# A recurrent layer's small weights: resident in plain fp32 instead of reloaded and split, and the spill of low parts moved to another issuing engine

## The chip, the cores and the metric

The kernel runs on one core of one Trainium2 chip. The metric is the device time of one execution in microseconds (us), the median of three runs of the kernel. A profile is one further execution with the hardware profiler on; its span (first to last instruction) lies inside its own time, and all durations and waits below come from that one execution.

The engines are named as the profile names them: PE is the matrix engine (PEld its weight loads), DVE, ACT and POOL are the three elementwise engines, SP issues transfers. ACT issues transfers as well, and those stand in its own instruction stream, between its computations. Every engine takes its instructions strictly in its own order: an instruction that waits for a semaphore holds everything behind it.

## The reference, cut to what matters

Two layers run over 1024 tokens of width 1024: first RWKV-7 time mixing, then sparse attention, each followed by a gated feed-forward part. The change touches only the first:

```python
xx = token_shift(x) - x
xm = x[None] + xx[None] * mix[:, None, None, :]
r, k, v = jnp.einsum('nbsd,nde->nbse', xm[:3], w_rkv)
xw, xa, xg = xm[3], xm[4], xm[5]
w_log = -jax.nn.softplus(-(w0 + jnp.tanh(xw @ w1) @ w2)) - 0.5
decay = jnp.exp(-jnp.exp(w_log.astype(f32)))
a = jax.nn.sigmoid(a0 + (xa @ a1) @ a2)
g = jax.nn.sigmoid(xg @ g1) @ g2
...
_, y = lax.scan(_wkv7_step, state0, xs)
```

`w2` and `a2` are the second low-rank weights: 64 rows by 1024 columns each. All of it is fp32.

## The kernel before, in words

**Products.** An fp32 operand of a large product is split into a high part (a cast to fp32r) and a low part (operand minus high part); `mm3` (L63) then makes one product out of three fp32r matmuls, high·high, high·low and low·high. Each split is one cast on ACT (L54) and one subtraction on DVE or POOL (L60). A plain fp32 matmul is also possible and needs no split; in the trace it stands as two matmul records for each instruction.

**The recurrent layer** (`rwkv`, L307) handles four units: two halves of 512 tokens (hf 0 and 1) times two groups of 512 channels (g 0 and 1). For a unit come, by the list `CFG['order']` at L867: the transposed input and the first low-rank products (`load_x`, `lora1`, once for each half), the second low-rank products (`lora2`), the projections r, k and v (`rproj`, `kproj`, `vproj`), the decays, the preparation and inversion of the chunks (`prep`, `invert`), and the recurrence over eight chunks (`wkv`). The recurrence of one unit is interleaved with the projections of the next; the first unit's projections have no recurrence beside them. A scheduler of the language then fixes the order on each engine from these calls.

**A projection** (`proj`, L471) runs over eight blocks of 128 input channels (kt 0 to 7). For each it needs the split weight block (`wh`, `wl`) and the split mixed input (`xmh`, `xml`), 128x512 each, and makes 12 matmuls of 512 columns: four output tiles times three. `pair` (L440) decides where operands come from. What is needed again is spilled to DRAM when it is first made and loaded when it is needed again: weights in hf 0 (`kept_w`), mixed inputs at g = 0 (`kept_xm`). So the first unit makes and spills both, the second makes and spills weights and loads mixed inputs, the third loads weights and makes and spills mixed inputs, the fourth only loads. A block moves 256 KB in each transfer: in the first unit one load and four spills. Both spills of a pair are issued by ACT (L451), high part then low part.

**Buffers.** Raw weight blocks pass through three tiles (`raw`, L395). All split operands pass through one ring of `k.NU` tiles (`u`, L317), 14 of 128x512: a tile is free for its next owner when its matmuls have run and its spill has landed. Four PSUM tiles (`acc`, L326) hold the outputs of a projection or of the low-rank products.

**`lora1`** (L398) makes four first low-rank products and from them `hw` (tanh, split: high part in rows 0 to 63, low part in rows 64 to 127) and `ha` (rows 0 to 63 and 64 to 127 as well), three DVE and three ACT instructions for the two. **`lora2`** (L500) loads the group's halves of `w2` and `a2` (stored twice, one copy for each 64 rows, so 128 rows each), splits them, and for each of four blocks of 128 channels makes two products of two 128-row fp32r matmuls (L517, L518) and applies a sigmoid on ACT (L519). It runs four times, once for each unit.

**Names in the rows below.** `pa` is the PSUM output of a projection, `la` of a first and `l` (`l2`) of a second low-rank product; `wr` is a raw weight block; `xm` the mixed input before its split; SPq and ACTq are the transfer issues of SP and ACT.

Of the kernel before, what the change touches and what calls it, by code (L numbers as in the profile page):

```python
# [7 lines left out]
F32 = mybir.dt.float32  # L8
F32R = mybir.dt.float32r
BF16 = mybir.dt.bfloat16  # L10
AF = mybir.ActivationFunctionType
ALU = mybir.AluOpType
# [12 lines left out]
V_MIX, V_W0, V_A0, V_KK, V_KA, V_RK = 0, 48, 56, 64, 72, 80  # L25
# [20 lines left out]
def f32(ap):  # L46
    return ap.bitcast(F32)
# [72 lines left out]
def wsplit(k, u, ap, n=512, lo_eng="v", raw=None):  # L120

    raw = (raw or u)("wr")[:, :n]
    lo, hi = u("wl", F32R)[:, :n], u("wh", F32R)[:, :n]
    k.nc.sync.dma_start(raw, ap)
    split(k, raw, hi, lo, "a", lo_eng)
    return hi, lo
# [180 lines left out]
def rwkv(k, src, dst):  # L307
    nc, tc = k.nc, k.tc
    E = lambda n: nc.vector if CFG[n] == "v" else nc.gpsimd
    pools = Pools(tc)  # L310
    P_, M_ = pools.add("rw", first=True, side="left"), pools.add("rwm", side="left")
# [5 lines left out]
    def u(name, dt=F32):  # L317
        return P_.tile([128, 512], dt, name=name, tag="u", bufs=k.NU)

    def t(name, dt=F32):  # L320
        return M_.tile([128, 512], dt, name=name, tag="t", bufs=5)
# [4 lines left out]
    def acc(name):  # L326
        return PS.tile([128, 512], F32, name=name, tag="acc", bufs=4)
# [25 lines left out]
    SB = [M_.tile([128, 4, 2, 64], F32, name=f"S{g}") for g in range(2)]  # L353
    for z in SB:
        nc.gpsimd.memset(z, 0.0)
    halo = M_.tile([128, 8], F32, name="halo")
    nc.gpsimd.memset(halo, 0.0)
    st = {}
# [33 lines left out]
    def wtile(ap, n=512, lo_eng="v"):  # L392
        return wsplit(k, u, ap, n, lo_eng, raw)

    def raw(name):  # L395
        return P_.tile([128, 512], F32, name=name, tag="raw", bufs=3)

    def lora1(hf):  # L398
        xT = st[hf]["xT"]
        a = [acc("la") for _ in range(4)]  # L400
        for kt in range(KT):
            xx = t("xx")
            nc.vector.tensor_tensor(xx, xT[:, kt, 0:512], xT[:, kt, 1:513], ALU.subtract)
            w = raw("wl1")[:, :288]
            nc.sync.dma_start(w, k.w_l1[kt * 128 : (kt + 1) * 128, :])
            xm = {}
            for n in (3, 4, 5):
                xm[n] = u("xm")
                c = V_MIX + 8 * n + kt
                nc.vector.scalar_tensor_tensor(  # L410
                    xm[n], xx, k.vec[:, c : c + 1], xT[:, kt, 1:513], ALU.mult, ALU.add
                )

            for b, n, c0, c1, p0 in ((0, 3, 0, 64, 0), (1, 4, 64, 128, 64), (2, 5, 128, 256, 0), (3, 5, 256, 288, 96)):
                nc.tensor.matmul(
                    a[b][p0 : p0 + c1 - c0], w[:, c0:c1], xm[n], start=kt == 0, stop=kt == KT - 1
                )
        hw = M_.tile([128, 512], F32R, name="hw", tag="hw", bufs=1)
        tw = t("tw")
        nc.scalar.activation(tw[:64], a[0][:64], AF.Tanh)  # L420
        nc.scalar.copy(hw[:64], tw[:64])
        nc.vector.tensor_tensor(hw[64:], tw[:64], f32(hw[:64]), ALU.subtract)
        ha = M_.tile([128, 512], F32R, name="ha", tag="ha", bufs=1)
        nc.scalar.copy(ha[64:], a[1][64:])
        nc.vector.tensor_copy(ha[:64], a[1][64:])
        nc.vector.tensor_tensor(ha[64:], a[1][64:], f32(ha[64:]), ALU.subtract)
        tg = t("tg")
        nc.scalar.activation(tg, a[2], AF.Sigmoid)
        nc.sync.dma_start(gsc[hf, 0:128], tg)
        tg2 = t("tg2")  # L430
        nc.scalar.activation(tg2[96:], a[3][96:], AF.Sigmoid)
        nc.sync.dma_start(gsc[hf, 128:160], tg2[96:])
        st[hf].update(hw=hw, ha=ha)

    ahead = {}
    PF = [CFG['pf0'], CFG['pf1'], CFG['pf2']]
# [1 line left out]
    kept = {}  # L438

    def pair(key, make, again):  # L440

        if key in kept:
            hi, lo = u(key[0] + "h", F32R), u(key[0] + "l", F32R)
            for i, x in enumerate((hi, lo)):
                nc.sync.dma_start(f32(x), kept[key][i])
            return hi, lo
        hi, lo = make()
        if again:
            kept[key] = DR.tile([2, 128, 512], F32, name="kept_" + "_".join(map(str, key)))
            for i, x in enumerate((hi, lo)):  # L450
                nc.scalar.dma_start(kept[key][i], f32(x))  # L451
        return hi, lo

    def operands(hf, n, g, kt):
# [11 lines left out]
    def prefetch(hf, n, g, m):  # L466

        for kt in range(m):
            ahead[hf, n, g, kt] = operands(hf, n, g, kt)
# [23 lines left out]
    def slot(ap, x):  # L493

        return ap.rearrange("p (c x i) -> p c x i", x=2, i=64)[:, :, x, :]

    def v2(ap):
        return ap.rearrange("p (c i) -> p c i", i=64)

    def lora2(hf, g):  # L500

        h_ = st[hf]
        AR = P_.tile([128, 4, 1024], F32, name="AR", tag="AR", bufs=2)
        BK = P_.tile([128, 4, 1024], F32, name="BK", tag="BK", bufs=1)
        s = un[hf, g] = dict(AR=AR, BK=BK)
        if CFG["pfl"] == "b":
            prefetch(hf, 0, g, 1)
        w2 = wtile(k.w_w2[:, g * 512 : (g + 1) * 512], lo_eng=CFG["l2"])
        a2 = wtile(k.w_a2[:, g * 512 : (g + 1) * 512], lo_eng=CFG["l2"])
        if CFG["pfl"] == "a":  # L510
            prefetch(hf, 0, g, 1)
        for i in range(4):
            p = 4 * g + i
            sl = slice(i * 128, (i + 1) * 128)
            for o, w, h, v0 in ((v2(BK[:, i, :512]), w2, h_["hw"], V_W0), (slot(AR[:, i], 0), a2, h_["ha"], V_A0)):
                ps = acc("l2")
                nc.tensor.matmul(ps, w[0][:, sl], h, start=True, stop=False)  # L517
                nc.tensor.matmul(ps, w[1][:, sl], h, start=False, stop=True)  # L518
                s["last"] = nc.scalar.activation(o, v2(ps), AF.Sigmoid, bias=k.vec[:, v0 + p : v0 + p + 1])  # L519

    def decays(hf, g):
# [345 lines left out]
    for j in range(-1, 5):  # L867
        for o in order:
            n, i = o[0], j + int(o[1:])
# [1060 lines left out]
def setup(tc, args, es):  # L1930
    k = Ctx()
    k.tc, k.nc = tc, tc.nc
    for n, a in zip(_INS, args):
        setattr(k, n, a)
    k.NU = 14
    k.psum = k.rows = None
    k.dram = es.enter_context(tc.tile_pool(name="scratch", bufs=1, space=bass.MemoryType.DRAM))
    C = es.enter_context(tc.tile_pool(name="consts", bufs=1, reuse_waits="tile"))
    k.ident = C.tile([128, 128], F32, name="ident")
    k.nc.sync.dma_start(k.ident, k.c_ident)  # L1940
    k.vec = C.tile([128, V_END], F32, name="vec")
    k.nc.sync.dma_start(k.vec, k.vecs)
    k.mhalf = C.tile([128, 16], F32, name="mhalf")
    k.nc.gpsimd.memset(k.mhalf, -0.5)
    return k
# [41 lines left out]
```

## Time and profile before

| what | value |
|---|---|
| time, median of 3 runs | 3228.42 us (3226.88 to 3240.63) |
| the profiled execution's own time | 3233.26 us |
| its span | 3231.4 us |
| mean granted clock of PE | 0.924 |
| PE busy | 2864.5 us, 89% |
| DVE busy | 2455.2 us, 76% |
| POOL busy | 1518.1 us, 47% |
| ACT busy | 1377.4 us, 43% |
| first matmul of the first unit's r projection | 51.55 us |
| last chunk output of the recurrence (L747) | 946.5 us |

A row of a group ("L60 POOL ... xml<-xm,xmh ... x42 | 57.6, 1372 | 125.4 <-ACT ...") gives line, engine, output and inputs, count, then busy us and mean ns of one, then the engine's idle time just before them and what ended it. A row of a timeline gives start and length in us, engine, line, output and inputs, and in brackets the idle time before it with its releaser. A row of waits gives the waiting instruction, what it waited for, and total us, number of times, longest. A window row gives for each engine busy us (and instructions) in a stretch, then the granted PE clock, the busy share of the 16 DMA engines, and GB/s.

### The profile page before, as it was taken

How to read it: one execution, taken by the hardware profiler on the slowest of the kernel's cores; microseconds unless marked ns; L12 is line 12 of the kernel's file. 1: busy time of each engine (PE TensorE's matmuls, PEld its weight loads, DVE VectorE, ACT ScalarE, POOL GpSimd, SP SyncE). 2: the span in 40 equal slices, each digit the busy share in tenths (PEclk: the TensorE clock that was granted, in tenths of full speed). 3: DMA queues.
4: the chain of work that ended last, by engine and by line, in shares of the span. 5: the costliest groups of instructions: out<-in, count | busy, mean ns of one | idle time of the engine just before them, and what ended most of it. 6: DMA issues, size and time to landing. Idle time of an engine off the chain costs nothing. (4 is left out here: it accounts for less than half of the span.)

```text
span 3231.4 us, 41664 instructions
## 1 busy us (share of the span) xinstructions
PE 2864.5 (89%) x15032; PEld 2246.0 (70%) x15032; DVE 2455.2 (76%) x3925; ACT 1377.4 (43%) x2363; POOL 1518.1 (47%) x987
## 2 busy tenths in 40 slices
PE   7689889989897899999698888888998899999788
PEld 3468657777675677777576766566787677777577
DVE  5486767766756788888976689997475888888975
ACT  3433234322322544444223577775363544444331
POOL 2433215222144667766767522212313677766766
PEclk9788978879898999999889889999999999999899
DMA  5554533534325222235212521112214222235212
GB/s 178 198 199 141 189 108 113 181 135 161 121 86 179 82 79 79 78 92 207 78 66 73 182 69 54 45 33 101 80 43 163 61 78 79 79 98 202 78 52 91
DMA packets 236224, 356.44 MB, mean 110 GB/s; under 512 B 17290, under 2 KB 110858, under 8 KB 235634
## 3 DMA queue, kind: packets, MB, share of 16 engines
q1 hardware_dynamic: 208370, 303.44, 29.3%
q10 hardware_dynamic: 27648, 50.34, 4.1%
q8 instruction: 118, 1.93, 0.3%
q14 instruction: 88, 0.72, 0.1%
HBM read 250.57 MB, written 103.15 MB: 109 GB/s over the span
## 5 line engine op out<-in xcount | busy, mean ns | idle before, releaser
L60 POOL TENSOR_TENSOR wo<-wr,wo 128x512 fp32r<-128x512 f32 x220 | 410.8, 1891 | 288.8 <-ACT wo L54 288.8
L1050 DVE SCALAR_TENSOR_TENSOR cv<-u,vec,cv 128x1023 f32<-128x1023 f32 (+1 forms) x176 | 348.2, 1996 | 52.9 <-ACT cv L1045 51.1
L65 PE MATMUL dn<-dh 128*128 128x512 f32 x532 | 219.4, 412 | 68.5 <-DVE acc L1177 68.4
L60 POOL TENSOR_TENSOR dl<-raw,dh 128x1024 fp32r<-128x1024 f32 x82 | 221.1, 2719 | 101.4 <-ACT dh L54 101.1
L65 PE MATMUL p<-xT,wo 128*128 128x512 f32 x528 | 213.4, 404 | 25.3 <-ACT u L1034 19.0
L66 PE MATMUL dn<-dl,dh 128*128 128x512 f32 x532 | 218.1, 410 | 15.2 <-POOL dl L60 7.7
L67 PE MATMUL dn<-dh,dl 128*128 128x512 f32 x532 | 215.9, 406 | 0.0
L1045 ACT ACTIVATE cv<-u,vec 128x1024 f32<-128x1024 f32 x88 | 109.5, 1244 | 248.8 <-DVE u L1039 248.2
L1682 POOL TENSOR_TENSOR cm<-sc,toep 128x256 f32<-128x256 f32 x96 | 75.7, 794 | 297.1 <-DVE mn L1698 228.5
L67 PE MATMUL p<-xT,wo 128*128 128x512 f32 x528 | 208.7, 395 | 5.1 <-POOL wo L60 5.1
L66 PE MATMUL p<-xT,wo 128*128 128x512 f32 x528 | 208.6, 395 | 3.0 <-DVE xT L60 3.0
L1177 DVE SCALAR_TENSOR_TENSOR acc<-acc,dn 128x512 f32<-128x512 f32 x196 | 130.8, 679 | 86.7 <-PE dn L67 86.7
L60 POOL TENSOR_TENSOR wo<-S,wo 128x512 fp32r<-128x512 f32 x88 | 175.6, 2014 | 30.3 <-ACT wo L54 30.3
L54 ACT CAST dh<-raw 128x1024 fp32r<-128x1024 f32 x95 | 94.8, 1047 | 198.0 <-PE dn L67 80.7
L65 PEld LDWEIGHTS dn<-dh 128*128 128x128 f32 x532 | 105.7, 199 | 98.0 <-DVE acc L1177 42.5
L60 POOL TENSOR_TENSOR wl<-wr,wh 128x512 fp32r<-128x512 f32 x56 | 76.6, 1367 | 199.2 <-ACT wh L54 118.5
L65 PEld LDWEIGHTS p<-xT,wo 128*128 128x128 f32 x528 | 100.6, 190 | 63.6 <-ACT u L1034 34.2
L65 PE MATMUL p<-x,wo 128*128 128x512 f32 x352 | 138.8, 394 | 2.8 <-DVE x L60 2.3
L54 ACT CAST wo<-wr 128x512 fp32r<-128x512 f32 x220 | 127.0, 618 | 29.1 <-POOL wo L60 18.7
L54 ACT CAST wh<-wr 128x512 fp32r<-128x512 f32 x108 | 66.6, 621 | 169.8 <-DMA wr<-in_w_w_dram 51.6
L66 PE MATMUL p<-x,wo 128*128 128x512 f32 x352 | 138.4, 393 | 0.0
L65 PE MATMUL pa<-xmh,wh 128*128 128x512 f32 x256 | 106.1, 439 | 36.3 <-ACT xmh L54 32.2
(422 smaller groups left out, 8685.9 us busy)
## 6 DMA issues: line engine op xcount, KB each, us to landing
wr<-in_w_up_dram SPq DMA_DIRECT2D x88, 512.0 KB, 5.9
hd<-cv SPq DMA_DIRECT2D x44, 512.0 KB, 3.4
raw<-hd SPq DMA_DIRECT2D x19, 1024.0 KB, 5.0
raw<-in_w_down_dram SPq DMA_DIRECT2D x19, 1024.0 KB, 7.7
wr<-in_w_wo_dram SPq DMA_DIRECT2D x68, 256.0 KB, 2.9
wr<-in_w_rkv_dram SPq DMA_DIRECT2D x48, 256.0 KB, 3.4
kept_w<-wh ACTq DMA_DIRECT2D x48, 256.0 KB, 2.2
kept_w<-wl ACTq DMA_DIRECT2D x48, 256.0 KB, 3.7
```

The costliest lines, as they stand in the source:

```text
L54: nc.scalar.copy(hi, raw)
L60: eng.tensor_tensor(lo, raw, f32(hi), ALU.subtract)
L65: mm(ps, lhs[0], rhs[0], start=start, stop=False, **kw)
L66: mm(ps, lhs[0], rhs[1], start=False, stop=False, **kw)
L67: mm(ps, lhs[1], rhs[0], start=False, stop=stop, **kw)
L1045: nc.scalar.activation(o, u, AF.Identity, bias=k.vec[:, cb : cb + 1], scale=k.vec[:, cw[2] : cw[2] + 1])
L1050: nc.vector.scalar_tensor_tensor(o[:, d:], u[:, : 1024 - d], k.vec[:, cw[j] : cw[j] + 1], o[:, d:], ALU.mult, ALU.add)
L1177: nc.vector.scalar_tensor_tensor(o, o, ALPHA if first else 1.0, ps, ALU.mult, ALU.add)
L1682: (nc.vector if CFG["cm"][h4] == "v" else nc.gpsimd).tensor_tensor(cm[:, :near], mk, toep[g][:, h % 8, 256 - near :], ALU.add)
```

## The change

Four edits go together.

1. `w2` and `a2` are loaded once at the start into one resident tile `wa2` (rows 0 to 63 hold `w2`, rows 64 to 127 hold `a2`, all 1024 columns), with no split. The eight loads of 256 KB inside `lora2` and their casts and subtractions go.
2. `lora1` makes one unsplit tile `h` (rows 0 to 63 the tanh, rows 64 to 127 the copy), two ACT instructions in all. `lora2` makes each product as one plain fp32 matmul over 64 rows: eight in place of sixteen 128-row fp32r matmuls.
3. In `pair` the high part is still spilled from ACT, the low part from SP.
4. The ring `u` has 13 tiles in place of 14, which makes room for `wa2`.

```diff
+    wa2 = M_.tile([128, 1024], F32, name="wa2")
+    nc.sync.dma_start(wa2[:64], k.w_w2[:64])
+    nc.sync.dma_start(wa2[64:], k.w_a2[64:])
...
-        hw = M_.tile([128, 512], F32R, name="hw", tag="hw", bufs=1)
-        tw = t("tw")
-        nc.scalar.activation(tw[:64], a[0][:64], AF.Tanh)
-        nc.scalar.copy(hw[:64], tw[:64])
-        nc.vector.tensor_tensor(hw[64:], tw[:64], f32(hw[:64]), ALU.subtract)
-        ha = M_.tile([128, 512], F32R, name="ha", tag="ha", bufs=1)
-        nc.scalar.copy(ha[64:], a[1][64:])
-        nc.vector.tensor_copy(ha[:64], a[1][64:])
-        nc.vector.tensor_tensor(ha[64:], a[1][64:], f32(ha[64:]), ALU.subtract)
+        h = M_.tile([128, 512], F32, name="h", tag="h", bufs=1)
+        nc.scalar.activation(h[:64], a[0][:64], AF.Tanh)
+        nc.scalar.copy(h[64:], a[1][64:])
...
             for i, x in enumerate((hi, lo)):
-                nc.scalar.dma_start(kept[key][i], f32(x))
+                (nc.scalar, nc.sync)[i].dma_start(kept[key][i], f32(x))
...
-        w2 = wtile(k.w_w2[:, g * 512 : (g + 1) * 512], lo_eng=CFG["l2"])
-        a2 = wtile(k.w_a2[:, g * 512 : (g + 1) * 512], lo_eng=CFG["l2"])
...
-            for o, w, h, v0 in ((v2(BK[:, i, :512]), w2, h_["hw"], V_W0), (slot(AR[:, i], 0), a2, h_["ha"], V_A0)):
+            for o, q, v0 in ((v2(BK[:, i, :512]), slice(0, 64), V_W0), (slot(AR[:, i], 0), slice(64, 128), V_A0)):
                 ps = acc("l2")
-                nc.tensor.matmul(ps, w[0][:, sl], h, start=True, stop=False)
-                nc.tensor.matmul(ps, w[1][:, sl], h, start=False, stop=True)
+                nc.tensor.matmul(ps, wa2[q, 128 * p : 128 * p + 128], h_["h"][q], start=True, stop=True)
...
-    k.NU = 14
+    k.NU = 13
```

How the order on the engines changes, at three places.

On ACT, in the middle of the first unit's r projection (blocks 3 and 4; `kept_w_0_0_3` is the spilled weight of projection 0, group 0, block 3), before:

```order
L54 CAST wh_478<-wr_476 128x512
L387 ACTIVATE xm_609<-xT_135,omm_127 128x512
L451 DMA kept_w_0_0_3_482<-wh_478 128x512
L451 DMA kept_w_0_0_3_482<-wl_477 128x512
L54 CAST xmh_487<-xm_485 128x512
L451 DMA kept_xm_0_0_3_492<-xmh_487 128x512
L451 DMA kept_xm_0_0_3_492<-xml_486 128x512
L54 CAST wh_509<-wr_507 128x512
```

and after:

```order
L54 CAST wh_455<-wr_453 128x512
L390 ACTIVATE xm_555<-xT_138,omm_127 128x512
L448 DMA kept_w_0_0_3_459<-wh_455 128x512
L54 CAST xmh_464<-xm_462 128x512
L390 ACTIVATE xm_586<-xT_138,omm_127 128x512
L448 DMA kept_xm_0_0_3_469<-xmh_464 128x512
L54 CAST wh_486<-wr_484 128x512
```

The two issues whose source is a low part (`wl`, `xml`) have left ACT's stream; before, each stood ahead of the next cast.

On SP at the same place, before, only weight loads stand in the queue:

```order
L124 DMA wr_445<-in_w_rkv_dram 128x512
L124 DMA wr_476<-in_w_rkv_dram 128x512
L124 DMA wr_507<-in_w_rkv_dram 128x512
L124 DMA wr_538<-in_w_rkv_dram 128x512
L124 DMA wr_569<-in_w_rkv_dram 128x512
```

and after, two low-part spills stand between one load and the next (blocks 1 to 3 are spilled, blocks 4 to 6 loaded):

```order
L448 DMA kept_w_0_0_1_397<-wl_392 128x512
L124 DMA wr_484<-in_w_rkv_dram 128x512
L448 DMA kept_xm_0_0_1_407<-xml_401 128x512
L448 DMA kept_w_0_0_2_428<-wl_423 128x512
L124 DMA wr_515<-in_w_rkv_dram 128x512
L448 DMA kept_xm_0_0_2_438<-xml_432 128x512
L448 DMA kept_w_0_0_3_459<-wl_454 128x512
L124 DMA wr_546<-in_w_rkv_dram 128x512
```

A load of block k+3 now stands behind the spill of the low weight of block k and of the low input of block k-1.

On SP in the second unit's r projection, where mixed inputs are loaded back, before:

```order
L445 DMA xmh_2208<-kept_xm_0_0_0_399 128x512
L445 DMA xml_2209<-kept_xm_0_0_0_399 128x512
L124 DMA wr_2274<-in_w_rkv_dram 128x512
L124 DMA wr_2299<-in_w_rkv_dram 128x512
L445 DMA xmh_2233<-kept_xm_0_0_1_430 128x512
L445 DMA xml_2234<-kept_xm_0_0_1_430 128x512
```

and after:

```order
L442 DMA xmh_2165<-kept_xm_0_0_0_376 128x512
L448 DMA kept_w_0_1_0_2162<-wl_2157 128x512
L442 DMA xml_2166<-kept_xm_0_0_0_376 128x512
L124 DMA wr_2206<-in_w_rkv_dram 128x512
L442 DMA xmh_2190<-kept_xm_0_0_1_407 128x512
L448 DMA kept_w_0_1_1_2187<-wl_2182 128x512
L442 DMA xml_2191<-kept_xm_0_0_1_407 128x512
```

The load of a block's `xml` now stands behind the spill of the same block's `wl`. In the third unit it is the load of the next block's `wl` that stands behind the spill of an `xml`.

More of the change, by code (lines that the diff above doesn't have):

```diff
@@ L432, in lora1 @@
         nc.sync.dma_start(gsc[hf, 128:160], tg2[96:])
-        st[hf].update(hw=hw, ha=ha)
+        st[hf].update(h=h)
     ahead = {}
@@ L505, in lora2 @@
         s = un[hf, g] = dict(AR=AR, BK=BK)
-        if CFG["pfl"] == "b":
-            prefetch(hf, 0, g, 1)
-        w2 = wtile(k.w_w2[:, g * 512 : (g + 1) * 512], lo_eng=CFG["l2"])
-        a2 = wtile(k.w_a2[:, g * 512 : (g + 1) * 512], lo_eng=CFG["l2"])
-        if CFG["pfl"] == "a":
-            prefetch(hf, 0, g, 1)
         for i in range(4):
             p = 4 * g + i
-            sl = slice(i * 128, (i + 1) * 128)
-            for o, w, h, v0 in ((v2(BK[:, i, :512]), w2, h_["hw"], V_W0), (slot(AR[:, i], 0), a2, h_["ha"], V_A0)):
+            for o, q, v0 in ((v2(BK[:, i, :512]), slice(0, 64), V_W0), (slot(AR[:, i], 0), slice(64, 128), V_A0)):
                 ps = acc("l2")
-                nc.tensor.matmul(ps, w[0][:, sl], h, start=True, stop=False)
-                nc.tensor.matmul(ps, w[1][:, sl], h, start=False, stop=True)
+                nc.tensor.matmul(ps, wa2[q, 128 * p : 128 * p + 128], h_["h"][q], start=True, stop=True)
                 s["last"] = nc.scalar.activation(o, v2(ps), AF.Sigmoid, bias=k.vec[:, v0 + p : v0 + p + 1])
```

## The prediction

> **What bounds the kernel now.** I read the windows by stage first, then the waits of PE and ACT in the stretch that looked worst, then the timeline of that stretch. The stretches are: second low-rank products of the first unit (40 to 51.5 us), its r projection, the decays, its k projection, its v projection with the chunk preparation, and then units two to four beside the recurrence.
>
> ```profile
> 40.00:51.50 11.50, 4.69 (x17) 2.60 (x16) 4.12 (x6) 10.20 (x17) 1.26 (x1) 1.00 0.35 115
> 51.50:95.30 43.80, 33.01 (x108) 22.19 (x108) 19.05 (x20) 20.53 (x34) 18.68 (x16) 0.88 0.76 264
> 95.30:109.00 13.70, 0.00 (x0) 0.00 (x0) 8.38 (x11) 6.93 (x13) 8.37 (x10) 0.65 0.17 58
> 109.00:141.30 32.30, 25.27 (x84) 17.02 (x84) 10.77 (x12) 13.02 (x22) 15.66 (x12) 0.88 0.79 269
> 141.30:203.20 61.90, 56.55 (x296) 43.65 (x297) 42.56 (x59) 23.46 (x40) 21.72 (x15) 0.81 0.51 177
> 214.00:430.00 216.00, 193.51 (x1419) 139.71 (x1417) 154.84 (x241) 64.19 (x109) 59.06 (x52) 0.89 0.48 160
> 430.00:950.00 520.00, 472.70 (x3832) 384.05 (x3833) 358.34 (x568) 172.82 (x288) 153.68 (x130) 0.86 0.38 130
> ```
>
> In the r and k projections no engine is full: PE is busy 33.0 of 43.8 and 25.3 of 32.3 us, ACT and POOL less than half, the DMA engines 0.76 and 0.79. That is a chain of waits. From 214 us on PE is busy nine tenths of the time, so nothing there can give much. The waits from 51.5 to 203 us, of PE and then of ACT:
>
> ```profile
> PE pa L65 <- ACT xmh L54: 29.8, 14, 13.8
> PE pa L66 <- POOL xml L60: 7.2, 11, 2.4
> ```
>
> ```profile
> ACT wh L54 <- POOL xml L60: 26.0, 16, 2.8
> ACT xmh L54 <- DVE wl L60: 8.6, 5, 4.8
> ACT xmh L54 <- DMA kept_w<-wh: 7.3, 4, 1.9
> ACT xmh L54 <- POOL wl L60: 5.9, 5, 1.3
> ```
>
> PE waits for casts on ACT, and ACT's casts wait for low parts that they do not read: 26.0 + 8.6 + 5.9 = 40.5 us. What stands between is the spill of the low part. One block of the r projection on ACT:
>
> ```profile
> 66.43 0.62 ACT L54 CAST wh<-wr 128x512 fp32r<-128x512 f32 x1 [1.81 <-POOL xml L60]
> ...
> 67.08 0.33 ACTq L451 DMA_DIRECT2D kept_w<-wh  x1
> 68.46 0.36 ACTq L451 DMA_DIRECT2D kept_w<-wl  x1
> 68.86 0.62 ACT L54 CAST xmh<-xm 128x512 fp32r<-128x512 f32 x1 [1.18 <-PE pa L67]
> 69.51 0.33 ACTq L451 DMA_DIRECT2D kept_xm<-xmh  x1
> 70.92 0.33 ACTq L451 DMA_DIRECT2D kept_xm<-xml  x1
> 71.29 0.62 ACT L54 CAST wh<-wr 128x512 fp32r<-128x512 f32 x1 [1.82 <-POOL xml L60]
> ```
>
> The cast at 66.43 is followed by the next block's at 71.29: a beat of 4.86 us. In it ACT stands from 67.41 to 68.46 and from 69.84 to 70.92 for the low part alone. POOL in turn begins a subtraction only after the cast: the two engines take turns.
>
> **The change part by part.**
>
> *Start.* Two more loads of 256 KB stand ahead of the eight input loads. While those ran:
>
> ```profile
> 5.00:10.00 5.00, 3.69 (x16) 3.02 (x16) 0.82 (x2) 1.18 (x2) 0.00 (x0) 1.00 0.96 296
> ```
>
> 0.524 MB at 296 GB/s is 1.8 us, and the first transposes wait for inputs, so I take all of it: +1.8 (between 0 and +2.5, if the extra issues hold up the later ones).
>
> *Second low-rank products of the first unit.* PE, then ACT:
>
> ```profile
> 14.92 25.23 PE L415 MATMUL la<-xm,wl 128*64 128x512 f32 x64 [1.99 <-issue]
> ...
> 44.72 0.39 PE L517 MATMUL l<-hw,wh 128*128 128x512 f32 x1
> 44.96 0.39 PE L518 MATMUL l<-hw,wl 128*128 128x512 f32 x1
> ...
> 51.55 0.64 PE L65 MATMUL pa<-xmh,wh 128*128 128x512 f32 x1 [4.53 <-ACT xmh L54]
> ```
>
> ```profile
> 41.92 0.59 ACT L431 ACTIVATE tg<-la 32x512 f32<-32x512 f32 x1
> ...
> 46.67 0.71 ACT L519 ACTIVATE AR<-l,vec 128x512 f32<-128x512 f32 x1
> 47.24 0.72 ACT L519 ACTIVATE BK<-l,vec 128x512 f32<-128x512 f32 x1
> ```
>
> A split product is two matmuls 0.24 us apart, 0.48 us. A plain fp32 product with a full 128 rows is two records; 32 of them took 25.23 us, 0.79 each. The 64-row form with 512 columns is not in the trace. Its nearest rows are 128 columns wide: products on alternating 64-row halves (L630), and full-height ones (L719).
>
> ```profile
> L630 PE MATMUL aps<-AR,BK 64*128 64x128 f32 x512 | 57.3, 293 | 7.5 <-DVE MA L632 7.5
> ...
> L719 PE MATMUL sps<-S,AR 128*128 128x128 f32 x256 | 41.8, 307 | 0.0
> ```
>
> 57.3/512 is 0.112 us a record against 41.8/256 = 0.163: halves cost 0.69 of full height. So eight products are 8 x 0.79 x 0.69 = 4.4 us by the nearest row, 6.3 at most, against 16 x 0.24 = 3.8 before. Here that is hidden: PE can start when the first products end at 40.15 rather than wait for a split of the tanh, and ACT's sigmoids, 0.57 us apart, follow the last gate sigmoid at 42.5. The eighth product needs the PSUM tile of the fourth sigmoid, at 42.5 + 4 x 0.57 + 0.57 for a mixed-input step between them = 45.4. So the r projection starts at about 46.4 rather than 51.55: -5.1.
>
> [...]
>
> *The r projection.* The waits for low parts go. What is late next: ACT has two casts, one mixed-input step and two issues, under 2.5 us; POOL two subtractions; PE twelve matmuls, 12 x 0.24 = 2.9 us; and the transfers. A block moves 5 x 262,144 bytes = 1.31 MB. The window moved 264 GB/s at share 0.76, so 347 at 1.0, and 1.31/347 is 3.8 us: transfers become the bound, not PE. At 0.95, as in the loads at the start, the window is 43.8 x 0.76/0.95 = 35.0 us: -8.8. The last block is not bound by them:
>
> ```profile
> 84.19 0.50 PE L65 MATMUL pa<-xmh,wh 128*128 128x512 f32 x1 [1.10 <-ACT xmh L54]
> 87.13 0.79 PE L66 MATMUL pa<-xml,wh 128*128 128x512 f32 x1 [2.44 <-POOL xml L60]
> ...
> 109.04 0.79 PE L65 MATMUL pa<-xmh,wh 128*128 128x512 f32 x1 [13.79 <-ACT xmh L54]
> ```
>
> There the subtraction stands behind the decays' work on POOL, whose order is unchanged. I take -8 (between 0 and -11, the idle PE in the window). The 13.8 us after it, in which ACT works on the decays, stay.
>
> *The k projection.* The same: 32.3 x 0.79/0.95 = 26.9, at most -5.4. I take -4, since the first two blocks are already prepared in the decays' time. *The v projection:* 61.9 - 56.6 = 5.3 us of idle PE; I take -3 (between 0 and -5).
>
> *Units two to four.* Low-rank products: +0.6 each by the nearest row (-0.6 to +2.5), less the earlier start in unit three. Two casts and two DVE subtractions go from each unit, three DVE instructions and one on ACT from each half: off the path. I take +1 in all (-3 to +7). Spills on SP:
>
> ```profile
> PE pa L65 <- DMA xmh<-kept_xm: 3.6, 3, 1.7
> ```
>
> ```profile
> ACT xmh L54 <- POOL xml L60: 10.9, 6, 3.6
> ```
>
> ACT is freed of 10.9 us of waits that PE mostly does not see; in exchange SP's loads wait for low parts, with one ring tile less. PE waited 3.6 us for these loads, so they have little to spare. I take 0 (between -5 and +34, priced below).
>
> Sum: +1.8 - 5.1 - 8 - 4 - 3 + 1 + 0 = -17.3 us. The profiled execution took 3233.26 us (span 3231.4), 4.8 above the median of 3228.42; the terms are differences, so I apply them to the median: 3211 us. This case's own range is 3198 to 3220.
>
> **The rivals.**
>
> *A. The transfers are the bound already; about no change.* If a mix of loads and spills does not go above the 0.79 of the k projection, the beat in r and k stays and the spill waits only move to a landing wait. Left are +1.8 - 5.1 - 3 + 1 = -5: 3223 us (3215 to 3229). For it: four ACT waits, 7.3 us, were for a spill's landing. Against it: in 67.41 to 68.46 ACT stands although nothing keeps the data from moving. [...]
>
> *B. PE also keeps its clock; 3197 us.* The matmul at 87.13 takes 0.79 where the one at 84.19, before the gap, takes 0.50; the v projection runs at 0.81. If fewer gaps keep the clock full there, 56.55 x 0.19 = 10.7 us go, and about 3 at the r projection's end: -17 - 14 = -31. Against it: the 13.8 us gap at the decays stays, and the half clock follows it. [...]
>
> *C. SP's queue holds its loads; slower.* In unit two the load of `xml` stands behind the spill of `wl` of the same block. With 13 tiles a block's tiles come free when the third block before it ends. Then cast, subtraction, load:
>
> ```profile
> L54 ACT CAST wh<-wr 128x512 fp32r<-128x512 f32 x82 | 50.5, 620 | 136.0 <-DMA wr<-in_w_w_dram 51.6 <-POOL xml L60 27.8 <-DMA wr<-in_w_wo_dram 19.2
> ```
>
> ```profile
> L60 POOL TENSOR_TENSOR wl<-wr,wh 128x512 fp32r<-128x512 f32 x40 | 56.0, 1399 | 162.5 <-ACT wh L54 94.8 <-PE zt L135 27.6 <-PE wo L66 24.7
> ```
>
> ```profile
> xml<-kept_xm SPq DMA_DIRECT2D x48, 256.0 KB, 3.8
> ```
>
> 0.62 + 1.40 + 3.8 plus two issues of 0.35 = 6.5 us, against two blocks of PE, 24 x 0.24 = 5.8: short by 0.7 where blocks run back to back. In 48 blocks (units two and three) that is 34 us, less the gain: +17, 3245 us. It decides from 0.36 us a block on (17.3/48). Against it: interleaved with the recurrence, 24 blocks of unit two share 216 us, 9 us each, which covers the chain.
>
> **How the numbers follow.** Forecast 0.50, A 0.22, B 0.13, C 0.15. Half a per cent of the median is 16.1 us, about what a measurement of this kernel can tell from no change. The forecast lies on that border: 0.33 of its 0.50 I count as faster, 0.17 as same. With B faster is 0.46; with A same is 0.39; slower is C, 0.15. The range takes in A, most of B, and the nearer half of C: 3190 to 3240.
>
> **What would show it.** Right: the beat in the r projection falls to about 4 us, its DMA share rises towards 0.95, ACT's waits for `xml` and `wl` there vanish, and the first r matmul comes near 48 us (46.4 + 1.8). Wrong towards A: a beat above 4.6 us with DMA share under 0.85. Wrong towards C: PE's waits for loads of `kept_xm` and `kept_w` grow from a few us to over 17.

## The result, and the profile after

The changed kernel takes 3177.98 us (median of four executions; 3170.01 to 3183.57) against 3227.65 us (four as well) for the kernel before on the same chip: a ratio of 0.9837, 95% interval 0.9801 to 0.9874, or 50 us less. The forecast was 17 us less and a range that began at 3190. The profiled execution after has a span of 3168.0 us against 3231.4 before. These two executions lie 63 us apart, since the one before was above its median and the one after below; stage times from them overstate the gain by about a quarter.

The windows by stage of the kernel after, with its own bounds: second low-rank products of the first unit, r projection, the wait for the decays, k projection, v projection with the chunk preparation. The columns are those of the prediction: busy time and number of records of PE, PEld, DVE, ACT and POOL, then granted PE clock, DMA share and GB/s.

```profile
41.60:47.60 6.00, 5.84 (x17) 2.07 (x16) 0.75 (x1) 5.94 (x11) 0.00 (x0) 1.00 0.54 184
47.60:82.30 34.70, 28.18 (x109) 19.42 (x108) 25.76 (x21) 22.70 (x38) 23.01 (x17) 1.00 0.90 323
82.30:93.50 11.20, 0.00 (x0) 0.00 (x0) 7.83 (x8) 5.25 (x9) 8.39 (x9) 0.71 0.17 56
93.50:117.15 23.65, 22.55 (x84) 17.50 (x84) 16.15 (x15) 14.23 (x24) 17.82 (x13) 0.85 0.90 329
117.15:173.68 56.53, 50.23 (x298) 39.29 (x297) 45.78 (x61) 23.87 (x42) 22.78 (x17) 0.94 0.61 213
```

At 12 products a block, the 108 of the r window are the eight blocks of r and the first of k, and the 84 of the k window are the other seven; it is so before and after. The r window is 34.7 us long for 43.8, the wait for the decays 11.2 for 13.7, the k window 23.65 for 32.3, the v projection with the preparation 56.5 for 61.9. The DMA share is 0.90 in r and in k. The first unit's low-rank products start 0.8 us later than before, and those of unit two 29.6 us earlier (173.7 for 203.25).

The timeline of ACT in the r projection after; the two numbers are start and duration:

```profile
52.94 0.60 ACT L54 CAST wh<-wr 128x512 fp32r<-128x512 f32 x1
...
55.21 0.60 ACT L54 CAST wh<-wr 128x512 fp32r<-128x512 f32 x1
...
56.34 0.60 ACT L54 CAST xmh<-xm 128x512 fp32r<-128x512 f32 x1
...
57.26 0.33 ACTq L448 DMA_DIRECT2D kept_xm<-xmh  x1
57.83 0.60 ACT L54 CAST wh<-wr 128x512 fp32r<-128x512 f32 x1
...
60.89 0.62 ACT L54 CAST xmh<-xm 128x512 fp32r<-128x512 f32 x1 [1.26 <-DMA kept_xm<-xml]
...
64.71 0.62 ACT L54 CAST xmh<-xm 128x512 fp32r<-128x512 f32 x1 [2.14 <-DMA kept_xm<-xml]
...
72.84 0.62 ACT L54 CAST wh<-wr 128x512 fp32r<-128x512 f32 x1
```

No issue of a low part stands between the casts any more. At first the beat is 2.3 to 2.6 us (52.94, 55.21, 57.83 for the casts of `wh`); later the cast waits until a low part's spill has landed and its ring tile is free (1.26 and 2.14 us in the rows, with the DMA engines 0.90 busy over the window). That is the transfer bound, and over six blocks (casts of `wh` at 52.94 and 72.84) the beat is 3.3 us for 4.86. On PE the eight blocks of r took 30.0 us (47.6 to 77.6), 3.7 each, near the 3.8 that the prediction worked out for the transfers of a block.

Units two to four together, up to the last product of the recurrence, in one window: before, then after.

```profile
203.20:946.50 743.30, 671.43 (x5284) 527.82 (x5283) 519.75 (x824) 243.68 (x406) 213.72 (x183) 0.87 0.42 139
```

```profile
173.70:881.70 708.00, 650.91 (x5279) 504.56 (x5278) 507.14 (x814) 235.12 (x396) 213.35 (x180) 0.91 0.43 144
```

35 us went here, where the prediction had +1; unit three alone went from 207.6 to 188.1 us. PE is busy 20.5 us less and idle 14.8 us less, with nearly the same number of matmul records (5284 and 5279), and the clock is 0.91 for 0.87. Time multiplied by clock is 647 us before and 644 after, which agree within the rounding of the clock (some 4 us): by that product the stage took the same number of clock pulses. From there to the end the two executions differ by 1.4 us.

Where the clock goes in unit three is seen in the timeline of PE around the inversion of unit two, whose 32x32 products (`xps`, `tps`) wait for transposes on DVE. Before, then after:

```profile
459.93 2.67 PE L678 MATMUL xps<-TX,MA 32*32 32x32 f32 x64 [3.27 <-DVE TX L666]
...
465.81 3.62 PE L683 MATMUL tps<-MA,TX 32*32 32x32 f32 x64
```

```profile
412.12 2.21 PE L667 MATMUL xps<-TX,MA 32*32 32x32 f32 x64
...
416.07 2.21 PE L672 MATMUL tps<-MA,TX 32*32 32x32 f32 x64
```

Before, PE runs out of projection products and waits 3.27 us in front of the first `xps`; after, it does not wait there. The same 64 `tps` products then take 3.62 us before and 2.21 after. 36 us in windows, before from the last products ahead of the wait, after from the first `xps`:

```profile
456.00:492.00 36.00, 32.73 (x351) 27.66 (x351) 15.87 (x19) 8.30 (x14) 2.55 (x2) 0.57 0.24 79
```

```profile
412.00:448.00 36.00, 35.60 (x502) 30.44 (x502) 24.42 (x28) 17.31 (x28) 11.70 (x11) 1.00 0.44 146
```

PE is busy 32.7 of 36 us in the one, at a clock of 0.57, and 35.6 in the other, at 1.00. At half clock for (1 - 0.57) x 36 / 0.5 = 31 us, and from 461.7 to 492.0 us the granted clock is 0.50: a wait of 3.27 us was followed by ten times its length at half clock, although PE had work. That the wait caused it is argued so far; experiments 5 and 7 bear on it.

### The profile page after: what moved, and what is told of

Its sections match the earlier page's. It is cut to its first block, busy times and chain, and to the rows that moved or that the text cites. A ratio compares the mean times of both kernels' runs of the same rounds, so it can differ in the third digit from the quotient of the medians.

```text
span 3168.0 us, 41686 instructions
## 1 busy us (share of the span) xinstructions
PE 2834.0 (89%) x15032; PEld 2217.4 (70%) x15032; DVE 2463.5 (78%) x3911; ACT 1368.9 (43%) x2353; POOL 1528.7 (48%) x987
## 5 line engine op out<-in xcount | busy, mean ns | idle before, releaser
L65 PE MATMUL p<-x,wo 128*128 128x512 f32 x352 | 138.9, 394 | 3.4 <-DVE x L60 3.0
L67 PE MATMUL p<-x,wo 128*128 128x512 f32 x352 | 138.4, 393 | 0.0
L66 PE MATMUL p<-x,wo 128*128 128x512 f32 x352 | 138.4, 393 | 0.0
L66 PEld LDWEIGHTS dn<-dl,dh 128*128 128x128 f32 x532 | 106.5, 200 | 38.4 <-DVE dl L60 8.4
```

Source lines behind the costliest of these rows:

```text
L65: mm(ps, lhs[0], rhs[0], start=start, stop=False, **kw)
L66: mm(ps, lhs[0], rhs[1], start=False, stop=False, **kw)
L67: mm(ps, lhs[1], rhs[0], start=False, stop=stop, **kw)
```

## The experiments

The kernel before had medians from 3223 to 3231 us in the groups of runs that follow; each ratio is to the runs of before beside it. Changed kernels of different groups are compared by their medians, and differences between them of less than some 8 us say little.

My theories after the result. **Theory 1:** everything came from the spills: the wait in front of a low part's issue held ACT, and the clock followed the gaps that went. **Theory 2:** the spills gave the first unit's gain and the low-rank edit that of units two to four. **A third** was that the smaller ring brought a luckier order of instructions.

**1. The spills alone.** The kernel before with one line changed:

```
-                nc.scalar.dma_start(kept[key][i], f32(x))
+                (nc.scalar, nc.sync)[i].dma_start(kept[key][i], f32(x))
```

> The kernel before, with one edit: low parts spilled from SyncE. Theory 1 (the spill wait on ACT is the cost, and the PE clock follows from the gaps that go): nearly the whole gain of 50 us, so 3178 to 3190 us; r projection with a beat near 3.9 us and about 35 us long, k projection near 24 us, PE clock over 0.9 in units two and three. Theory 2 (the spills give only what was forecast for the first unit, and the low-rank products give what units two to four gained): 3205 to 3215 us, unit three still near 207 us at a clock of 0.83. In both the r projection still starts near 51.5 us.

3198.74 us, ratio 0.9907 (0.9884 to 0.9930): 30 us less, neither theory's number. Its r and k projection, and units two to four, in windows:

```profile
50.50:83.60 33.10, 28.23 (x108) 20.76 (x108) 24.92 (x21) 20.42 (x34) 23.85 (x18) 0.95 0.99 358
94.90:118.90 24.00, 22.86 (x85) 17.71 (x85) 16.32 (x15) 14.19 (x24) 17.35 (x13) 0.84 0.91 330
```

```profile
175.60:912.10 736.50, 675.27 (x5284) 532.87 (x5282) 520.25 (x824) 242.75 (x405) 215.12 (x183) 0.86 0.42 141
```

The first unit is the changed kernel's: unit two starts at 175.6 (173.7 there). Units two to four are near those of before (736.5 us, clock 0.86), unit three at 0.84. Theory 1 falls; of theory 2 the places hold, not the size.

**2. The low-rank edit alone.** The changed kernel with that line undone, so with the ring of 13 tiles.

```
-                (nc.scalar, nc.sync)[i].dma_start(kept[key][i], f32(x))
+                nc.scalar.dma_start(kept[key][i], f32(x))
```

> The changed kernel with low parts spilled from ScalarE again, so only the resident weights, the plain products and the ring of 13 tiles are left. Theory 1: within 10 us of the kernel before (3218 to 3232), r projection starting near 47.6 us but with the old beat of 4.8 us. Theory 2: 3195 to 3205 us, with unit three near 190 us.

3209.09 us, ratio 0.9939 (0.9914 to 0.9963), between the ranges of the two theories. The first r product comes at 50.97, not near 47.6, and unit two starts at 203.3, as before; units two to four are 21 us shorter:

```profile
203.30:925.40 722.10, 661.06 (x5279) 513.77 (x5278) 506.65 (x815) 236.29 (x397) 211.38 (x180) 0.89 0.42 141
```

By the ratios the two edits are worth 30 and 20 us, together the 50 measured: they add up, each mainly in its own place. Unit three fell from 207.6 to 191.9 us.

**3. The ring alone.** In the kernel before:

```
-    k.NU = 14
+    k.NU = 13
```

> The kernel before with 13 ring tiles for 14, and nothing else. Theories 1 and 2: within 8 us of the kernel before, either sign. A third theory, that the gain is an accident of a new order of instructions from the smaller ring: 20 us or more faster.

3238.24 us, ratio 1.0031 (1.0014 to 1.0048), 10 us slower. The third theory falls. If the effects add, the low-rank edit brings some 30 us, of which its ring tile takes 10 back.

**4. PE kept busy through the decays.** The changed kernel with, behind the first r projection:

```
+        if (hf, g) == (0, 0):
+            with tc.issue_after(k.mm.ins):
+                for _ in range(12):
+                    k.warm = nc.tensor.matmul(mi("warm"), k.ident, smask, start=True, stop=True)
```

A second edit, not shown, puts all of the first unit's k projection behind these products.

> The changed kernel with 12 matmuls added behind the first unit's r projection, identity times a constant, whose result nobody reads: about 9.5 us of PE work in the 11.3 us in which PE waits for the decays, and nothing else moved. If the half clock at the start of the k projection comes from that gap, its first twelve matmuls come 0.23 us apart instead of 0.43, and the k projection is 2 to 3 us shorter, 21 us instead of 23.6; the total goes down by 2 to 3 us, unless the decays or the transfers set the k projection's pace, in which case the clock is full and the time the same. If the clock has another cause, the first twelve stay 0.43 apart and the time stays.

3171.82 us, ratio 0.9825 (0.9801 to 0.9849), not to be told from the changed kernel. In the timeline of PE the k projection's first products come 0.24 us apart (first two rows), at a granted clock of 1.00, where the changed kernel has 0.43 (the other two), at 0.50 from 93.5 to 100 us:

```profile
91.26 0.40 PE L66 MATMUL pa<-xml,wh 128*128 128x512 f32 x1
91.50 0.40 PE L67 MATMUL pa<-xmh,wl 128*128 128x512 f32 x1
```

```profile
95.98 0.63 PE L67 MATMUL pa<-xmh,wl 128*128 128x512 f32 x1
96.41 0.63 PE L65 MATMUL pa<-xmh,wh 128*128 128x512 f32 x1
```

So the gap did set that clock. Yet the k projection ends at the same 117.2. Its window is 26.6 us long for 23.7 because it holds one block more, 99 records for 84, three of them of the added products: the block that the changed kernel runs ahead of the decays stands behind the added products here. A block takes 3.3 us for 3.4, not the 2 to 3 us less in all that were expected; ACT's casts now wait for spills to land.

```profile
90.60:117.20 26.60, 23.98 (x99) 17.59 (x97) 17.81 (x16) 16.70 (x29) 19.96 (x15) 1.00 0.83 303
```

```profile
109.98 0.62 ACT L54 CAST xmh<-xm 128x512 fp32r<-128x512 f32 x1 [2.74 <-DMA kept_xm<-xml]
```

The same block explains why PE ends ahead of the decays at 77.2 here and at 82.3 in the changed kernel: r itself ends near 77.5 in both.

**5 and 6. Products in front of the inversion.** In the kernel before, and in the changed one, ahead of each unit's first `xps`:

```
+                if o == 0 and sub == 0:
+                    Lf = Lt.rearrange("p a b -> p (a b)")[:, :512]
+                    for _ in range(3):
+                        k.warm = nc.tensor.matmul(mi("warm"), k.ident, Lf, start=True, stop=True)
```

The `xps` of that step are held behind them; that line is not shown.

> The kernel before, with three matmuls (identity times the finished inverse, result read by nobody) ahead of the 32x32 matmuls of every unit's inversion, where PE waits 3.1 to 3.3 us for the transposes. Theory A (the part of the gain in units two to four is PE clock: a gap of over 3 us in front of the inversion halves the clock, and the small matmuls of the recurrence leave it at half for some 30 us): the stretch of half clock behind the inversion in units three and four is gone, unit three falls from 208 to near 192 us at a clock of 0.9, and the whole is 15 to 30 us faster than before. Theory B (the gain there is work and waits taken from VectorE and ScalarE, and the clock only goes with it): no faster than before, and up to 7 us slower for 9.5 us of added PE work.

3212.57 us, ratio 0.9971 (0.9954 to 0.9987), 9 us less than before (4 to 15; 13 by the medians): more than theory B allows and short of theory A's 15. Unit three took 199 us, where theory A had 192. Unit three's inversion on PE, 36 us with it, and units two to four:

```profile
452.41 2.08 PE L680 MATMUL warm<-Lt,ident 128*128 128x512 f32 x2 [4.56 <-DVE Lt L662]
...
457.74 2.21 PE L683 MATMUL xps<-TX,MA 32*32 32x32 f32 x64
```

```profile
444.00:480.00 36.00, 31.13 (x393) 23.70 (x393) 27.10 (x35) 11.59 (x20) 6.90 (x6) 0.91 0.35 121
205.60:922.50 716.90, 652.60 (x5284) 504.12 (x5282) 518.01 (x820) 241.78 (x404) 213.04 (x182) 0.90 0.43 144
```

The wait is still there (4.56 us now, in front of the added product), but behind the 128x512 products the clock is back (0.50 from 450 to 456 us, 1.00 from 458 to 480), the `xps` take 2.21 us, and the window stands at 0.91 for 0.57. Units two to four took 717 us for 743. Adding work to PE made the kernel faster, which speaks for the clock as a cause and not as something that goes along. It is not proof: the added products also hold back the instructions behind them, and a new order alone can move the stage by as much (experiment 12).

> The changed kernel with the same three matmuls ahead of each inversion. Theory A: unit two, whose wait there is 5.0 us with half clock from 210 to 234 us, gets 3 to 7 us shorter, unit four too, and the whole is 5 to 15 us faster than the changed kernel's 3178. Theory B: the same time, or up to 7 us slower.

3188.82 us, ratio 0.9888 (0.9868 to 0.9909): 11 us slower than the changed kernel, against theory A and beyond theory B's 7. Units two to four took 721 us for 708. The remedy did not carry over; whether a shifted order of instructions undid it is not separated.

**7. The old splits put back.** The changed kernel, its products untouched, with the loads, casts and subtractions of before for the weights and the activations, results unused:

```
+        wtile(k.w_w2[:, g * 512 : (g + 1) * 512], lo_eng=CFG["l2"])
+        wtile(k.w_a2[:, g * 512 : (g + 1) * 512], lo_eng=CFG["l2"])
```

and once per half:

```
+        tw = t("tw")
+        nc.scalar.copy(tw[:64], h[:64])
+        nc.vector.tensor_tensor(tw[64:], h[:64], tw[:64], ALU.subtract)
+        ta = t("ta")
+        nc.vector.tensor_copy(ta[:64], h[64:])
+        nc.vector.tensor_tensor(ta[64:], a[1][64:], h[64:], ALU.subtract)
```

> The changed kernel with the work of the old splits put back and its results left unused: per unit two loads, two casts on ScalarE and two subtractions on VectorE for the second low-rank weights, and per half the three VectorE instructions and one ScalarE copy for the activations; the products stay plain ones from the resident weights. If the low-rank gain of units two to four is that VectorE and ScalarE work, it is lost: 3195 to 3205 us, with unit three near 205 us. If the gain is the shape and order of the products on PE, it stays: 3175 to 3185 us, unit three near 190 us.

3208.40 us, ratio 0.9947 (0.9931 to 0.9964): 30 us slower than the changed kernel; the gain of the low-rank edit is gone. Units two to four, and two stretches of unit three from its inversion on:

```profile
182.60:925.10 742.50, 692.54 (x5279) 540.02 (x5279) 513.07 (x819) 240.14 (x404) 215.53 (x183) 0.85 0.43 140
```

```profile
450.70:454.10 3.40, 3.40 (x73) 3.14 (x73) 1.07 (x1) 1.68 (x3) 0.00 (x0) 1.00 0.68 231
454.10:474.50 20.40, 20.40 (x218) 18.08 (x218) 7.89 (x10) 5.13 (x9) 1.44 (x2) 0.50 0.16 53
```

PE's idle time is 742.5 - 692.5 = 50 us, less than the changed kernel's 57, and the stage is 34 us longer: there the loss is clock (0.85). Another 9 us lie in the first unit (unit two starts at 182.6 for 173.7). In both stretches of unit three PE is busy without a break, and yet the clock falls from 1.00 to 0.50 between them: a wait of PE is not needed for that.

**11, 14, 15. Which of the splits.** Each in the changed kernel: the activations' part alone; the weights' casts, subtractions and ring tiles without loads; the loads alone. The first is the second piece above; the others, in `lora2`:

```
+        for _ in range(2):
+            hi, lo = u("wh", F32R), u("wl", F32R)
+            split(k, wa2[:, g * 512 : (g + 1) * 512], hi, lo, "a", CFG["l2"])
```

```
+        for w in (k.w_w2, k.w_a2):
+            nc.sync.dma_start(raw("wr"), w[:, g * 512 : (g + 1) * 512])
```

> The changed kernel with only the activations' splits put back and left unused: three VectorE instructions and one ScalarE copy per half, no loads and no weight splits. With those and the weights' splits the gain of 30 us was lost. If what counts is VectorE work between the first low-rank products and the inversion of the unit before, a part of the loss shows here in unit three, 5 to 10 us, and none in units two and four: 3183 to 3190 us. If it is the weights' loads and splits that hold the queues, it stays at 3178 within 5 us.

> The changed kernel with the weights' splits put back without their loads: per unit two casts on ScalarE, two subtractions on VectorE and four tiles of the ring, from the resident weights, results unused. If engine work and ring tiles are what the old low-rank weights cost, most of the loss of the run with all splits back is here: 3192 to 3205 us. If it was the loads, whose cast stood at the head of ScalarE's queue until they landed, it stays within 6 us of 3178.

> The changed kernel with only the two loads of 256 KB per unit put back into the buffers that they had, read by nobody. If SyncE's queue and those buffers are the cost: 3190 us or more. If not: within 6 us of 3178.

3186.07 us (ratio 0.9880, 0.9843 to 0.9918), 3210.39 us (0.9927, 0.9906 to 0.9949) and 3184.59 us (0.9867, 0.9846 to 0.9888), beside 0.9837 for the changed kernel. The weights' casts, subtractions and ring tiles carry the loss; by the median it is all there, though the ten executions run from 3194 to 3220 us, and the runs don't tell casts from tiles. By the medians the loads cost 7 us and the activations' part 8, too little to tell from nothing. For the casts and tiles, units two to four:

```profile
179.10:923.20 744.10, 676.09 (x5280) 528.06 (x5279) 514.01 (x822) 239.13 (x402) 215.52 (x182) 0.87 0.42 137
```

**8. Both parts from SyncE.**

```
-                (nc.scalar, nc.sync)[i].dma_start(kept[key][i], f32(x))
+                nc.sync.dma_start(kept[key][i], f32(x))
```

> The changed kernel with the high parts spilled from SyncE too. If a queue that holds loads behind spills costs PE time (the rival of the prediction that ends slower), twice the spills stand ahead of the loads and PE's waits for loads in units two and three grow from about 5 us to over 15: 3190 us or more. If the loads have room, and ScalarE's own issue slots (0.33 us each) are off the path, the time stays within 8 us of 3178, with the r projection within 2 us of its 34.7 us.

3200.35 us, ratio 0.9925 (0.9896 to 0.9954), 22 us slower, but not by the loads of units two and three: PE's waits for them, below, are 8.6 us, not over 15. The first unit's k projection ended 9.3 us later than in the changed kernel (126.5 for 117.2). All its eight blocks (96 products) stand behind the decays here and took 40 us, where experiment 4 needed 26.6 for the same eight. In that execution units two to four were 16 us longer as well, 724 us at a clock of 0.88. PE's waits for loads in units two to four, then ACT's longest wait in the k projection, and its window:

```profile
PE pa L65 <- DMA xmh<-kept_xm: 6.1, 2, 4.6
...
PE pa L65 <- DMA wh<-kept_w: 2.5, 4, 0.8
```

```profile
ACT wh L54 <- DMA wr<-in_w_rkv_dram: 10.7, 3, 7.9
```

```profile
86.50:126.50 40.00, 31.39 (x96) 22.64 (x97) 24.20 (x23) 20.11 (x35) 25.19 (x20) 0.76 0.78 274
```

ACT's cast waits up to 7.9 us for a weight block, whose load stands on SP behind spills that wait in turn for a cast. That is the mechanism of the prediction's slower rival, at another place and with twice the spills.

**9 and 10. Loads later, ring of 12.** Each in the changed kernel: the two loads of the resident weights moved from the start to behind `lora1` of the first half; and a ring tile less.

```
                 lora1(un_[0])
+                if un_[0] == 0:
+                    nc.sync.dma_start(wa2[:64], k.w_w2[:64])
+                    nc.sync.dma_start(wa2[64:], k.w_a2[64:])
```

```
-    k.NU = 13
+    k.NU = 12
```

> The changed kernel with the two loads of the resident weights queued behind the eight input loads and three first weights; nothing else is moved. If the two loads ahead of the inputs cost the start what they take, the first transpose starts near 6.3 us instead of 8.4 and the r projection 2 us earlier, near 45.6 us. If the start is set by the fixed latency of the first load, it stays at 8.4. The whole time moves by less than can be measured either way.

> The changed kernel with 12 ring tiles for 13. One tile less cost the kernel before about 10 us. If the loads of units two and three sit that close to the edge, the third tile gone costs at least as much again: 3188 to 3200 us, with longer waits of PE for loads. If not, within 8 us of 3178.

3188.34 us (ratio 0.9890, 0.9857 to 0.9923) and 3185.74 us (0.9883, 0.9847 to 0.9920). The timeline of PE with the loads later, then of the changed kernel, then of the kernel before:

```profile
6.01 1.94 PE L372 MATMUL pt<-ident,xr 128*128 128x128 f32 x8 [6.01 <-DMA xr<-in_x_dram]
...
41.27 6.01 PE L505 MATMUL l<-h,wa 64*128 64x512 f32 x16
```

```profile
8.44 6.04 PE L374 MATMUL pt<-ident,xr 128*128 128x128 f32 x32 [8.44 <-DMA xr<-in_x_dram]
...
41.65 6.02 PE L507 MATMUL l<-h,wa 64*128 64x512 f32 x16
47.63 0.50 PE L65 MATMUL pa<-xmh,wh 128*128 128x512 f32 x1
```

```profile
6.29 1.94 PE L371 MATMUL pt<-ident,xr 128*128 128x128 f32 x8 [6.29 <-DMA xr<-in_x_dram]
...
40.84 0.50 PE L517 MATMUL l<-hw,wh 128*128 128x512 f32 x1 [0.69 <-DVE hw L422]
```

The first transpose comes 2.4 us earlier and the low-rank products only 0.4: what the loads take ahead of the inputs does not reach them. In the four executions with the old start (before, experiments 1, 3 and 5) these products begin between 40.84 and 43.31 us, so 0.4 can't be told from nothing. But units two to four took 18 us more in that execution, with the same products, and the median is 10 us higher; why is open.

```profile
175.40:901.80 726.40, 666.69 (x5279) 517.97 (x5278) 509.31 (x815) 235.38 (x396) 213.47 (x180) 0.88 0.43 140
```

The ring of 12 cost 8 us by the medians, inside the interval.

**12 and 13. The inversion earlier, and the changed kernel again.**

```
-'k0 r0 a0 A0 v0 x1 l0 l1 x0 d0 b0 i0 w0 W0 r1 d1'
+'k0 r0 a0 A0 v0 i0 x1 l0 l1 x0 d0 b0 w0 W0 r1 d1'
```

> The changed kernel with the inversion placed ahead of the next unit's low-rank stages in the order table, so that VectorE starts its chain earlier against PE's stock of products. No arithmetic is added or left out. If the wait in front of the inversion is what halves the clock in units two to four, PE's waits for the transposes fall from 14 us to under 6, the stretches of half clock behind them shrink, and units two to four together take 695 to 705 us instead of 708, the whole 5 to 15 us less than the changed kernel run beside it. If the clock is lost at other gaps as well, the half clock only moves to another place and the time stays within 5 us.

> The changed kernel once more, nothing altered, beside the one with the earlier inversion. If its time is a property of its order of instructions, its median is within 3 us of 3178 and units two to four take 708 us within 3. If where the clock is lost depends on how the gaps fall against the throttle's own timing, they spread over 708 to 726 us as in the two variants that have the same order (715.8 and 726.3), with the granted clock and not the product of time and clock moving.

3206.82 us (ratio 0.9929, 0.9904 to 0.9954) and 3176.78 us (0.9834, 0.9815 to 0.9854). Units two to four, the earlier inversion first, with PE's waits for a cast and for the transposes, those of the changed kernel, and the repeat:

```profile
179.50:927.30 747.80, 678.50 (x5279) 530.14 (x5278) 497.44 (x814) 236.11 (x396) 213.50 (x180) 0.87 0.41 136
```

```profile
PE pa L65 <- ACT xmh L54: 11.8, 1, 11.8
PE pa L66 <- DMA xml<-kept_xm: 8.7, 3, 6.2
PE xps L667 <- DVE TX L655: 7.6, 5, 5.0
```

```profile
PE xps L667 <- DVE TX L655: 14.1, 4, 7.0
```

```profile
177.30:882.60 705.30, 646.00 (x5279) 500.29 (x5278) 508.09 (x815) 235.24 (x396) 213.30 (x180) 0.92 0.44 144
```

The repeat agrees with the first run: the gain belongs to this kernel and isn't luck of one execution. The earlier inversion missed both outcomes that were expected of it: it halved PE's waits for the transposes (7.6 us for 14.1) and opened an 11.8 us wait for a cast and others for loads; the clock fell to 0.87 and units two to four took 748 us. So no single gap sets the clock there, and an order alone, with no work added, moved the stage by 40 us in that execution (29 us by the medians of the whole).

## Why the prediction was wrong, point by point

By the ratios, moving the spills gave 30 us, where their terms (-8, -4, -3 and 0) come to 15, and the low-rank edit with its ring tile gave 20, where its terms (+1.8, -5.1 and +1) come to 2.3.

**Start (+1.8).** The first transpose moved by 2.2 us (8.44 for 6.29), as forecast, but the second low-rank products by 0.8, and with the loads out of the way by 0.4. The term is under 1 us, less than the 2.5 us by which equal starts differ (experiment 9): the work between hid the rest.

**Second low-rank products of the first unit (-5.1).** Right for the changed kernel: the first r product came at 47.63 (48.0 in the repeat), and the forecast was near 48. Their records took 6.02 us, not the 4.4 that I took, with ACT busy 5.94 of the window's 6.00 us: its sigmoids set that pace. Where ACT did not, at the start of unit two, four products took 1.99 us, 0.50 each, against the 0.55 that I had taken from the nearest row:

```profile
173.68 1.99 PE L507 MATMUL l<-h,wa 64*128 64x512 f32 x8
```

Part of this gain does not hold from kernel to kernel: in experiments 2 and 10, with the same products, the first r product came at 50.97 and 50.37.

**r projection (-8).** Right: -9.1, with the beat down to 3.3 us, ACT's waits for low parts down from 15.1 to 0.7 us and the DMA share at 0.90. The issues alone, 2 x 0.35 us in each of 8 blocks, are 5.6 us; the r window of experiment 1 is 43.8 - 33.1 = 10.7 us shorter. So the wait in front of an issue goes as well.

**The decays (0).** -2.5: the wait was 11.2 us for 13.7. What shortened it isn't shown.

**k projection (-4, at most -5.4).** -8.7. The step that failed is the bound: it let all bytes of the window before, 32.3 us x 269 GB/s = 8.7 MB, pass within the k projection. After, 23.65 us x 329 GB/s = 7.8 MB pass there, and the v projection's window grew from 61.9 x 177 = 11.0 MB to 56.5 x 213 = 12.0 MB. Spills that nobody waits for moved on to a stage that had room.

**v projection (-3).** -5.4 in the profiled execution, but not by the step that I gave: the 3 us were to come out of PE's idle time, and that went from 5.3 to 6.3 us. All of the gain is clock, 0.94 for 0.81, which is the mechanism of the rival in which PE keeps its clock; I gave it 0.13 and looked for it in the first unit alone. It does not hold from one execution to the next either. In the repeat of the changed kernel (experiment 13) the same stage is 1.6 us shorter than before:

```profile
117.00:177.30 60.30, 55.37 (x297) 43.03 (x296) 45.25 (x60) 23.81 (x42) 23.03 (x17) 0.83 0.58 204
```

So where the clock fell in this stage was luck of that execution; the r, decays and k windows of the repeat agree with the first run (34.3, 11.2 and 23.5 us).

**Units two to four (+1, from -3 to +7).** This is the step that failed most: the removed casts and subtractions were written off as "off the path". Putting them back, with the products untouched, costs 30 us (experiment 7), and the weights' casts, subtractions and ring tiles alone cost as much (experiment 14). What the forecast left out is the clock: it took PE, busy nine tenths of the time, as full, although the rows that it showed have a clock of 0.89 and 0.86. Time x clock lies between 631 and 651 us in all seventeen profiled executions, the ones above and the rest, while the time runs from 705 to 749, so the difference is in the main granted clock. PE's idle time does not order them: it is 50 us with the splits back (742.5 us long) and 57 in the changed kernel (708). How the splits lower the clock stays open. In unit three of the kernel before, the half clock followed a wait of 3.27 us of PE for DVE, and 128x512 products put there gave 9 us back (experiment 5); in experiment 7 it also came without a wait (0.50 for 20.4 us with PE busy). Nor do the runs separate the engine time of the splits, their ring tiles and the other order of instructions that they bring about: an order alone did as much (experiment 12). No run shows the -0.6 us at the low end of what I allowed for a unit's low-rank products; at the 0.50 us measured above for a product, eight take 4.0 us, against 3.8 before.

**Spills on SP in units two and three (0), ring tile (within it).** PE's longest wait for their loads, from 170 to 900 us of the changed kernel:

```profile
PE pa L66 <- DMA xml<-kept_xm: 3.6, 2, 3.3
```

The loads had room: 3.6 us for the tile waited for most, as before, and 6.3 us for all of them, for 7.7 before. The slower rival did not come about; with both parts on SP its mechanism did, in the k projection. The ring tile cost 10 us in the kernel before, which I had put at nothing; this part of the sum was wrong the other way.

**Rival A**, transfers already the bound, falls: the share rose from 0.79 to 0.90 in the k projection.

## What to carry to other kernels

Where PE is busy nine tenths of the time, multiply a stage's time by its granted clock before writing it off as full: if the product is well below the time (here 647 of 743 us), there is time to win, and work on an engine that feeds PE can cost some of it without being what PE waits for (experiment 7: 34 us more at a clock of 0.85 for 0.91, with PE idle for 50 us and not 57). Look at that in more than one execution of the same kernel. Here a store whose source another engine still had to write held what was queued behind it on the issuing engine: ACT's waits for low parts in the r projection were 15.1 us, and 0.7 with the store on another queue. Give it to a queue with room, and no more than that queue has room for (both parts on SP cost 22 us). Stores that nobody reads soon need not count into a stage's transfer bound: of the 8.7 MB that I counted into the k projection, 7.8 passed there.

## What the hardware showed that I had not expected

Work on PE doesn't always bring the clock back, and a wait isn't needed to lose it. In experiment 7 PE was busy without a break from 450.7 to 474.5 us (the two window rows there). The clock was 1.00 up to 454.1 and 0.50 from there on; the 218 records of these 20.4 us took 0.09 us each on the mean, where a 128x512 product took 0.43 at half clock (experiment 4), so most of them were narrower. In experiment 5 the clock, 0.50 from 450 to 456 us, was back within 457.74 - 452.41 = 5.3 us after 128x512 products began, and the narrow products behind them then ran at 1.00 (64 `xps` in 2.21 us). In the changed kernel narrow products alone, with PE busy 7.90 us, kept the clock at 1.00 for 8.3 us, from 419.4 to 427.7. What decides whether they keep it or lose it is not shown.
